# Sliding-window attention of a two-layer encoder step: the split of the transposed probabilities of every first tile goes from VectorE to GpSimd

## The chip, the cores and the metric

One core of a Trainium2 chip runs one launch of the whole step. The metric is the device time of that launch in microseconds. The kernel is one static program: every engine has its own list of instructions, written out in advance, and works through it in order; engines wait for each other by semaphores only.

## The reference, cut to what matters

A step of an encoder with one mLSTM layer and one layer of sliding-window attention, each followed by a SwiGLU feed-forward part, over 1024 prompt rows and 32 sample rows. The change lies in the attention of the second layer:

```python
def sink_attention(q, k, v, sinks, bias):
    s = jnp.einsum('bcqhgd,bckhd->bchgqk', q, k).astype(F32) * (HEAD_DIM ** -0.5) + bias
    sk = sinks.astype(F32).reshape(N_KV_HEADS, GROUP)[:, :, None, None]
    mx = jnp.maximum(jnp.max(s, -1, keepdims=True), sk)
    p = jnp.exp(s - mx)
    p = p / (jnp.sum(p, -1, keepdims=True) + jnp.exp(sk - mx))
    return jnp.einsum('bchgqk,bckhd->bcqhgd', p.astype(v.dtype), v)
```

There are 16 query heads of 64 dimensions, 2 shared key/value heads, chunks of 64 rows, and a window of 192 keys. Everything is float32. TensorE multiplies in the rounded format fp32r, so the kernel splits each operand x into hi = round(x) and lo = x - hi, and multiplies both halves.

## The kernel before, in words

The attention is a static software pipeline over 72 tiles (j, b). j = 0..7 is a couple of query heads, b = 0..8 a block of 128 rows (b = 8 holds the 32 sample rows). Tiles (j, b) with j even and j + 1 with the same b form a pair; j even is the first tile of a pair. The order is by visits (jp, g), each visit being heads j = 2 jp and 2 jp + 1 and three blocks b: first all four jp with g = 0, then for each jp the two other groups. The last visits are (3, 1) and (3, 2), so the last twelve tiles are (6,3), (7,3), (6,4), (7,4), (6,5), (7,5), (6,6), (7,6), (6,7), (7,7), (6,8), (7,8).

A tile passes six stages:

- `scores` (lines 1881 to 1910): TensorE multiplies query halves with key halves into the bank psS (L1898); VectorE adds the bias and takes a minimum (L1904).
- `soft` (L1919): ScalarE takes the exponential and its sum.
- `scale`: VectorE takes the reciprocal (L1929); GpSimd multiplies the tile of 128x384 by it (L1932; blocks 0 and 8 have L1936 in its place).
- `turn` (lines 1946 to 1962): TensorE transposes the three 128x128 pieces into a PSUM bank T (L1957, two banks); ScalarE copies them, rounded, into hi (L1961); VectorE subtracts hi from T into lo (L1962).
- `values` (L1986): once per pair, TensorE multiplies hi and lo of both tiles with the values into the PSUM bank O (one bank).
- `place`: once per pair, ScalarE copies half of O (L2000), VectorE adds it into the activations (L2004).

`pipeline` (lines 106 to 130) fixes the order in which these are written into the engines' lists. In one round it tries `place`, `turn`, `scale`, `soft`, `scores`, `values`, in that order; `turn` runs three tiles behind `scale`, and `values` one tile behind `turn`. So a round that turns tile k next scales tile k + 3; the values of a pair are multiplied in the round that turns the first tile of the following pair, and placed in the round after it. Blocks 0 and 8 are split in two narrower cuts per tile.

Between these stages `Weave` puts other work, by pauses in microseconds written into the code: projections of queries (L435 to L437 into d, L1750 and L1753 split them into Q), the splitting of the attention output for the output projection (`split_act`, L465 rounds, L466 subtracts; for the first group of columns the rounding of even k and the subtraction of odd k are on GpSimd), the splitting of weights (`Weights._next`, L256 and L258 round, L260 subtracts; for the output projection of this layer some halves are on GpSimd), and the first tiles of the output projection (L1272). None of these pauses depends on what an engine really takes, so the order of the lists does not change with the change below.

Of the kernel before, what the change touches and what calls it, by code (L numbers as in the profile page):

```python
# [9 lines left out]
F32 = mybir.dt.float32  # L10
# [6 lines left out]
P = 128  # L17
# [287 lines left out]
def kernel(ctx: ExitStack, tc: tile.TileContext, A, O):  # L305
    nc = tc.nc
# [5 lines left out]
    def pool(name, space=None, side=None):  # L312
        kw = {}
        if space is not None:
            kw["space"] = space
        if side is not None:
            kw["side"] = side
        return tc.tile_pool(name=name, bufs=1, reuse_waits="tile", **kw)

    def new(p, tag, shape, dt=F32, bufs=1):  # L320
        uid[0] += 1
        return p.tile(list(shape), dt, name=f"{tag}_{uid[0]}", tag=tag, bufs=bufs)
# [1498 lines left out]
    pb2 = eb.enter_context(pool("pb2"))  # L1821
# [47 lines left out]
    def attention():  # L1869
# [68 lines left out]
        def blocks(b):  # L1938

            if b == 0:  # L1940
                return [(1, 130, 64), (2, 258, P)]
            if b == 8:
                return [(0, 2, P), (1, 130, DEC)]
            return [(t, 2 + t * P, P) for t in range(3)]

        def turn(j, b):
            s = S.pop((j, b))
            p = s["p"]
            rows = 2 * DEC if b == 8 else P
            if j % 2 == 0:  # L1950
                pairs_[j // 2, b] = {
                    tag: new(pb2, tag, [P, 2, 3, P], F32R, bufs=2) for tag in ("hi", "lo")
                }
            s = pairs_[j // 2, b]
            pt = new(psb, "T", [P, 512], bufs=2).rearrange("p (t r) -> p t r", t=4)
            for t, at, nk in blocks(b):
                nc.tensor.transpose(pt[:nk, t, :rows], p[:rows, at : at + nk], ident[:rows, :rows])  # L1957
            cuts = [(slice(0, 3), P)] if 0 < b < 8 else [(slice(t, t + 1), nk) for t, _, nk in blocks(b)]
            hi, lo = (s[x][:, j % 2] for x in ("hi", "lo"))
            for t, nk in cuts:  # L1960
                nc.scalar.copy(hi[:nk, t, :rows], pt[:nk, t, :rows])  # L1961
                nc.vector.tensor_sub(lo[:nk, t, :rows], pt[:nk, t, :rows], hi[:nk, t, :rows].bitcast(F32))  # L1962
# [25 lines left out]
        def place(j, b):  # L1988
# [12 lines left out]
            for h in range(2):  # L2001
# [10 lines left out]
                (soft, always, 0, 0),  # L2012
                (scale, always, 0, 0),
                (turn, always, 2, gaps[0]),
                (values, lambda j, b: ast["v"] > b, 1, gaps[1]),
                (place, always, 0, 0),
# [201 lines left out]
```

## Time and profile before

| | before |
|---|---|
| median of 3 runs | 2192.62 us (2192.11 to 2194.38) |
| profiled execution | 2192.83 us, of which the span of the trace is 2190.7 us |
| granted TensorE clock over the span | 0.998 of full speed |
| busy share of the span: PE, PEld, DVE, ACT, POOL | 99%, 98%, 66%, 45%, 41% |
| instructions | 44028 |

PE is the matrix multiply of TensorE, PEld its loading of weights, DVE is VectorE, ACT is ScalarE and POOL is GpSimd. Times in the rows are microseconds from the start of the span unless marked ns. The attention runs from about 1206 to 1406 us; nothing of the change lies outside of it.

### The profile page before, as it was taken

The numbers are of one execution on the slowest core, as the hardware profiler recorded it, in microseconds if no ns is written. First come the engines' busy times: TensorE is split into PE (matmuls) and PEld (weight loads), VectorE is DVE, ScalarE is ACT, GpSimd is POOL, SyncE is SP. The second block draws the span as 40 slices with busy tenths as digits, with TensorE's granted clock in tenths as the row PEclk, the third lists the DMA queues.
The fourth block names the chain that finished last, engine by engine and source line by source line (L and its number), as shares of the span: only waits on it lengthen the run. The fifth ranks groups of instructions, "written<-read, shape, count | busy, mean of one in ns | idle before, by whom it ended". The sixth has DMA issues, their size and how long they took to land.

```text
span 2190.7 us, 44028 instructions
## 1 busy us (share of the span) xinstructions
PE 2162.7 (99%) x16982; PEld 2136.5 (98%) x16982; DVE 1455.3 (66%) x2833; ACT 991.9 (45%) x2234; POOL 903.3 (41%) x926
## 2 busy tenths in 40 slices
PE   9999999999999999999999999999999999999997
PEld 9999999999999999999999999999999999999997
DVE  4465676778767666466657776888666666457657
ACT  4443355455444444322235777656444444422125
POOL 2544210003655655454421443501665655554441
PEclk9999999999999999999999999999999999999999
DMA  5221112212656555697517433511443433397712
GB/s 172 75 66 55 51 49 80 96 40 69 235 197 208 211 201 200 205 333 252 180 45 245 150 118 126 161 35 39 145 146 143 158 140 143 131 358 244 254 52 80
DMA packets 187361, 322.49 MB, mean 147 GB/s; under 512 B 18768, under 2 KB 124296, under 8 KB 187152
## 3 DMA queue, kind: packets, MB, share of 16 engines
q1 hardware_dynamic: 182800, 315.36, 43.1%
q10 hardware_dynamic: 4352, 4.33, 0.6%
q8 instruction: 134, 2.20, 0.4%
q14 instruction: 75, 0.61, 0.1%
HBM read 221.23 MB, written 96.57 MB: 145 GB/s over the span
## 4 chain that ended last, share of the span: by engine, by line
PE 86%; DVE 7%; ACT 3%; issue 1%; DMA 1%; POOL 0%; SPq 0%; DVEq 0%; ACTq 0%; POOLq 0%
PE d L435 10%; PE A L435 10%; PE A L437 10%; PE A L436 10%; PE d L437 10%; PE d L436 10%; PE B L435 7%; PE B L436 7%; PE B L437 7%; PE O L1986 1%; PE psS L1898 1%; PE T L1957 1%; DMA hs_x<-z 1%; ACT act L538 1%; PE T L988 1%
## 5 line engine op out<-in xcount | busy, mean ns | idle before, releaser
L260 POOL TENSOR_TENSOR wl_s<-wr,wh_s 128x512 fp32r<-128x512 f32 x224 | 304.2, 1367 | 241.2 <-ACT wh_s L258 181.4
L435 PE MATMUL d<-sx,wh 128*128 128x264 f32 (+2 forms) x1040 | 331.4, 319 | 0.2
L260 POOL TENSOR_TENSOR wl_a<-wr,wh_a 128x512 fp32r<-128x512 f32 x112 | 155.7, 1392 | 401.9 <-ACT wh_a L258 397.7
L437 PE MATMUL d<-sx,wl 128*128 128x264 f32 (+2 forms) x1040 | 316.2, 304 | 1.7 <-DVE wl L260 0.9
L436 PE MATMUL d<-sx,wh 128*128 128x264 f32 (+2 forms) x1040 | 315.7, 304 | 0.6 <-DVE sx L466 0.4
L435 PE MATMUL A<-sx,wh_s 128*128 128x264 f32 x896 | 254.5, 284 | 0.0
L436 PE MATMUL A<-sx,wh_s 128*128 128x264 f32 x896 | 254.2, 284 | 0.0
L437 PE MATMUL A<-sx,wl_s 128*128 128x264 f32 x896 | 254.0, 284 | 0.0
L258 ACT CAST wh_s<-wr 128x512 fp32r<-128x512 f32 x224 | 135.7, 618 | 192.1 <-DVE wr L201 102.9
L435 PEld LDWEIGHTS d<-sx,wh 128*128 128x128 f32 x1040 | 196.0, 188 | 3.6 <-ACT sx L465 0.4
L436 PEld LDWEIGHTS d<-sx,wh 128*128 128x128 f32 x1040 | 196.3, 189 | 1.9 <-DVE sx L466 1.1
L437 PEld LDWEIGHTS d<-sx,wl 128*128 128x128 f32 x1040 | 195.5, 188 | 2.4 <-DVE wl L260 1.4
L435 PE MATMUL d<-sx,ex 128*128 128x264 f32 x624 | 180.7, 290 | 0.1
L436 PE MATMUL d<-sx,ex 128*128 128x264 f32 x624 | 177.2, 284 | 0.0
L437 PE MATMUL d<-sx,ex 128*128 128x264 f32 x624 | 176.9, 284 | 0.0
L437 PEld LDWEIGHTS A<-sx,wl_s 128*128 128x128 f32 x896 | 168.8, 188 | 0.0
L435 PEld LDWEIGHTS A<-sx,wh_s 128*128 128x128 f32 x896 | 168.4, 188 | 0.2 <-issue 0.2
L436 PEld LDWEIGHTS A<-sx,wh_s 128*128 128x128 f32 x896 | 168.4, 188 | 0.0
L1396 POOL TENSOR_TENSOR z<-z 128x528 fp32r<-128x528 f32 x76 | 103.9, 1367 | 122.6 <-ACT z L1395 114.1
L435 PE MATMUL A<-ex,wh_s 128*128 128x264 f32 x448 | 127.5, 285 | 0.0
L436 PE MATMUL A<-ex,wh_s 128*128 128x264 f32 x448 | 127.1, 284 | 0.0
L437 PE MATMUL A<-ex,wl_s 128*128 128x264 f32 x448 | 127.1, 284 | 0.0
(377 smaller groups left out, 7126.6 us busy)
## 6 DMA issues: line engine op xcount, KB each, us to landing
wr<-in_gu SPq DMA_DIRECT2D x92, 512.0 KB, 4.4
hs_x<-z SPq DMA_DIRECT2D x72, 528.0 KB, 3.1
hs_t<-z SPq DMA_DIRECT2D x64, 528.0 KB, 4.7
sx<-hs_x SPq DMA_DIRECT2D x112, 264.0 KB, 5.9
sx<-hs_t SPq DMA_DIRECT2D x64, 264.0 KB, 6.1
ex<-hs_t SPq DMA_DIRECT2D x64, 264.0 KB, 6.0
wr<-in_dn SPq DMA_DIRECT2D x32, 512.0 KB, 4.9
wh<-halves SPq DMA_DIRECT2D x38, 256.0 KB, 3.2
```

Source lines behind the costliest of these rows:

```text
L258: self.nc.scalar.copy(hi, r)
L260: eng.tensor_sub(lo, r, hi.bitcast(F32))
L435: nc.tensor.matmul(out, ah, bh, start=start and k == 0, stop=False, **kw)
L436: nc.tensor.matmul(out, ah, bl, start=False, stop=False, **kw)
L437: nc.tensor.matmul(out, al, bh, start=False, stop=stop and k == last, **kw)
L538: nc.scalar.activation(z, z, AF.Identity, scale=gk, bias=bk)
L988: nc.tensor.matmul(pc[:, : 2 * (DV + 1)], keys, vt[j][:, c], start=True, stop=True)
L1396: eng.tensor_sub(lo.bitcast(F32R), buf(s), hi)
L1898: nc.tensor.matmul(ps[:rows, at : at + nk], lhs, k[:, k0 : k0 + nk], start=i == 0, stop=i == 1)
L1957: nc.tensor.transpose(pt[:nk, t, :rows], p[:rows, at : at + nk], ident[:rows, :rows])
L1986: nc.tensor.matmul(out, v[:nk], x, start=i == 0, stop=i == len(todo) - 1)
```

## The change

For the first tile of each pair, in blocks 1 to 7 (4 x 7 = 28 of the 72 tiles), ScalarE copies the transposed probabilities out of PSUM as plain float32 into a new SBUF buffer "tc" (one buffer of 128x384). GpSimd then rounds that buffer into hi and subtracts hi from it into lo. ScalarE's rounding copy and VectorE's subtraction of these tiles are left out. The second tile of each pair and blocks 0 and 8 stay as they were.

```diff
             cuts = [(slice(0, 3), P)] if 0 < b < 8 else [(slice(t, t + 1), nk) for t, _, nk in blocks(b)]
             hi, lo = (s[x][:, j % 2] for x in ("hi", "lo"))
+            if j % 2 == 0 and 0 < b < 8:
+                c = new(pb2, "tc", [P, 3, P])
+                nc.scalar.copy(c[:], pt[:, :3])
+                nc.gpsimd.tensor_copy(hi[:], c[:])
+                nc.gpsimd.tensor_sub(lo[:], c[:], hi[:].bitcast(F32))
+                return
             for t, nk in cuts:
                 nc.scalar.copy(hi[:nk, t, :rows], pt[:nk, t, :rows])
                 nc.vector.tensor_sub(lo[:nk, t, :rows], pt[:nk, t, :rows], hi[:nk, t, :rows].bitcast(F32))
```

## Rows read from the trace of the kernel before

**Rows 1.** The page, part 1: busy time and share of the span.

```profile
PE 2162.7 (99%) x16982; PEld 2136.5 (98%) x16982; DVE 1455.3 (66%) x2833; ACT 991.9 (45%) x2234; POOL 903.3 (41%) x926
```

**Rows 2.** Busy time by stretch: attention, its tail (stretch, length, PE, PEld, DVE, ACT, POOL, clock, DMA).

```profile
1206.00:1410.00 204.00, 197.83 (x1457) 188.25 (x1456) 152.00 (x601) 148.20 (x495) 94.90 (x151) 1.00 0.42 131
...
1376.00:1406.00 30.00, 28.94 (x233) 27.87 (x234) 26.88 (x82) 23.25 (x70) 22.85 (x25) 1.00 0.49 146
```

**Rows 3.** Waits of TensorE, 1206 to 1410: waited for, total us, times, longest.

```profile
PE O L1986 <- DVE act L2004: 1.8, 4, 0.7
...
PEld T L1957 <- POOL s L1932: 1.2, 1, 1.2
```

**Rows 4.** Groups by shape, GpSimd, 1206 to 1410 (busy us, mean ns, idle before).

```profile
L1932 POOL TENSOR_TENSOR s<-s,st 128x384 f32<-128x384 f32 x56 | 47.6, 852 | 77.5 <-DVE st L1929 56.1 <-DVE st L1904 8.7 <-ACT s L1919 5.8
L466 POOL TENSOR_TENSOR sx<-act,sx 128x384 fp32r<-128x384 f32 x8 | 8.1, 1012 | 3.2 <-ACT sx L465 3.1
...
L465 POOL CAST sx<-act 128x384 fp32r<-128x384 f32 x4 | 2.0, 502 | 0.0
```

**Rows 5.** Groups by shape, 1200 to 1420: the split of VectorE and ScalarE.

```profile
L1962 DVE TENSOR_TENSOR lo<-T,hi 128x384 fp32r<-128x384 f32 x56 | 31.1, 556 | 12.5 <-ACT hi L1961 11.7
...
L1961 ACT CAST hi<-T 128x384 fp32r<-128x384 f32 x56 | 26.5, 476 | 15.0 <-PE T L1957 14.4
```

**Rows 6.** Timeline of GpSimd in the tail (start, us, instruction, idle before it).

```profile
1378.91 1.32 POOL L1932 TENSOR_TENSOR s<-s,st 128x384 f32<-128x384 f32 x1
...
1384.37 2.07 POOL L1932 TENSOR_TENSOR s<-s,st 128x384 f32<-128x384 f32 x2
...
1387.94 0.83 POOL L1932 TENSOR_TENSOR s<-s,st 128x384 f32<-128x384 f32 x1 [0.53 <-DVE st L1929]
1389.05 0.83 POOL L1932 TENSOR_TENSOR s<-s,st 128x384 f32<-128x384 f32 x1 [0.28 <-PE d L436]
...
1395.14 2.06 POOL L1932 TENSOR_TENSOR s<-s,st 128x384 f32<-128x384 f32 x2
1397.16 0.80 POOL L466 TENSOR_TENSOR sx<-act,sx 128x288 fp32r<-128x288 f32 x1
```

**Rows 7.** Timeline of TensorE in the tail.

```profile
1386.17 0.49 PE L1957 MATMUL T<-ident,s 128*128 128x128 f32 x3
...
1396.47 0.55 PE L1957 MATMUL T<-ident,s 128*128 128x128 f32 x3 [0.98 <-POOL s L1932]
...
1397.58 0.28 PE L1986 MATMUL O<-hi,VR 128*128 128x256 f32 x1
...
1401.16 0.28 PE L1986 MATMUL O<-hi,VR 128*128 128x256 f32 x1
```

**Rows 8.** Timeline of GpSimd, two roundings that VectorE waits for.

```profile
1273.69 0.83 POOL L1932 TENSOR_TENSOR s<-s,st 128x384 f32<-128x384 f32 x1 [0.42 <-DVE st L1929]
1274.46 0.50 POOL L465 CAST sx<-act 128x384 fp32r<-128x384 f32 x1
...
1283.73 0.50 POOL L465 CAST sx<-act 128x384 fp32r<-128x384 f32 x1
```

**Rows 9.** Timeline of VectorE behind those two roundings.

```profile
1275.00 0.56 DVE L466 TENSOR_TENSOR sx<-act,sx 128x384 fp32r<-128x384 f32 x1 [0.94 <-POOL sx L465]
...
1284.26 0.56 DVE L466 TENSOR_TENSOR sx<-act,sx 128x384 fp32r<-128x384 f32 x1 [1.40 <-POOL sx L465]
...
1286.12 0.85 DVE L2004 TENSOR_TENSOR act<-O,t 64x256 f32<-64x256 f32 x2
```

**Rows 10.** Timeline of TensorE: the value products behind them.

```profile
1276.46 0.35 PE L1986 MATMUL O<-hi,VR 128*128 128x256 f32 x1 [0.72 <-DVE act L2004]
...
1287.56 0.28 PE L1986 MATMUL O<-hi,VR 128*128 128x256 f32 x1
```

**Rows 11.** Line 1986, all its instructions: the semaphore row (ns min/median/max).

```profile
L1986 PEldq EVENT_SEMAPHORE  x28: 51/51/51, 1225.9 to 1404.2; - x28
```

**Rows 12.** Line 260, a row of its instructions: ns min/median/max, first and last start.

```profile
L260 DVE TENSOR_TENSOR wl<-wr,wh x53: 660/684/1287, 5.0 to 1519.8; 128x512 fp32r<-128x512 f32 x53
```

## The prediction

> **What bounds the kernel now.** I read the busy table first: TensorE's multiplies are busy for 99% of the span [rows 1], so time can be won only where TensorE waits, and is lost wherever something makes it wait. The table by stretch then says how much that is in the attention: PE is busy 197.83 of 204 us, so 6.2 us of idle time are all that any relief of another engine could give back there. It also says who has room. Over the whole attention GpSimd is busy 94.90 us of 204, less than half. In the last 30 us it is busy 22.85, and VectorE 26.88 [rows 2]. An average over the attention would hide that tail.
>
> Next the waits of TensorE. They are short and come from several engines: the longest sum is the value products behind VectorE's addition of the pair before (1.8 us in 4 waits), and there is one wait of 1.2 us for GpSimd's scaling [rows 3]. That last one is at 1396.47 [rows 7], in the tail, and is the warning: there GpSimd is already the engine that ends last.
>
> **What the change removes.** 28 of the 56 VectorE subtractions of 128x384 at 0.556 us go: 28 x 0.556 = 15.6 us of VectorE. 28 ScalarE roundings at 0.476 us become 28 plain copies of the same shape out of the same bank [rows 5]; I take the same duration, so zero. T becomes free one step earlier, after ScalarE. What are the 15.6 us worth? At most the 6.2 us of idle PE. I looked at what VectorE did just ahead of each wait that it ended: an addition, the query split, a reduction, or the subtraction of the second tile of a pair, which stays. In none was it the removed one. I take 0, and allow up to 2 us for shifts that I did not see.
>
> **What it adds.** 28 roundings and 28 subtractions of 128x384 on GpSimd. Both shapes exist: 0.502 and 1.012 us [rows 4]. Together 1.51 us per pair and 28 x 1.51 = 42.4 us, so GpSimd goes from 94.9 to 137 of 204 us. It has room on average; the question is what stands behind the 1.51 us in its list. By the order of a round, that is the scaling of tile k + 3, when tile k is turned, and whatever weight or activation splitting is woven in there.
>
> In the steady part this is covered. The scaling is needed only three tiles later, and a pair takes about 200 / 36 = 5.5 us. GpSimd stood idle for 77.5 us just ahead of its scalings [rows 4], which takes the delay up. The halves of the first tile are used by the values of its pair a whole pair's time later. So 22 or 23 of the 28 cost nothing as long as that idle time stands.
>
> **First place where it does not: two roundings.** At 1274.46 and 1283.73 GpSimd rounds activations [rows 8] for a subtraction in which VectorE already waits 0.94 and 1.40 us [rows 9]. Behind it stands the addition that frees the bank O for the next value products. In the list the new work of tile (6,2) goes ahead of a scaling just before the first rounding, that of (0,7) ahead of the scaling just before the second. Only 0.42 us of idle stood there in the first case [rows 8], so the rounding moves by 1.51 - 0.42 = 1.1 us, and TensorE, already waiting at 1276.46 [rows 10], by the same. In the second the rounding moves by about 1.5, but the addition ended at 1286.12 + 0.85 = 1286.97 and the products began at 1287.56 [rows 9, 10]: 0.6 us of slack, so 0.9 us. Together 2.0 us. Bounds: 0, if the new pieces start early enough, to 3.
>
> **Second place: the tail.** From about 1377 on GpSimd runs nearly without a gap. The work of (6,3) goes in ahead of the scaling at 1378.91, that of (6,4) between the two scalings at 1384.37, that of (6,5) ahead of the scaling at 1389.05. Three pieces make 3 x 1.51 = 4.5 us. GpSimd's gaps on the way are 0.53 and 0.28 us [rows 6]. So the first scaling at 1395.14, of tile (6,7), comes 4.5 - 0.8 = 3.7 us later. TensorE waited for it already, 0.98 us at 1396.47 [rows 7], so nothing is left to cover it: 3.7 us. A part falls due earlier: the first of the two scalings at 1384.37 ended at 1384.37 + 2.07 / 2 = 1385.4 and would end at 1386.9, against its transposes at 1386.17, a stall of about 0.75 us inside the 3.7. Then the piece of (6,6) stands between the two scalings at 1395.14 (1.03 each) and ends at 1396.2 + 3.7 + 1.5 = 1401.4, against value products due at 1397.58 + 3.7 = 1401.3; that of (6,7) follows the second scaling, the subtraction at 1397.16 and a narrower scaling that I put at 0.8 too, and ends near 1401.4 + 1.0 + 0.8 + 0.8 + 1.5 = 1405.5, against products due at 1401.16 + 3.8 = 1405.0 [rows 6, 7]. With 0.1 and 0.4 us the tail comes to 4.2 us. Bounds: 2, if only the last wait counts and something behind takes it up, to 6, from the next part.
>
> **Beside GpSimd, VectorE.** An operation of GpSimd next to a VectorE operation with two SBUF operands is stretched on both sides in this trace: the scaling takes 0.85 us in the mean and 1.32 at 1378.91, the weight subtraction 0.684 in the median and 1.287 at most [rows 4, 6, 12]. The subtraction removed reads PSUM and one SBUF tile; so do VectorE's score reductions. The new GpSimd pieces are long and can meet the two-operand ones: five pieces in the tail at 0.4 us each would be 2 us more. [...] I keep 4.2, because the scaling's mean is far below 1.32, so most pieces should run undisturbed, and the removed subtractions shorten VectorE's list at the same places.
>
> **Semaphores.** The values now wait for GpSimd besides ScalarE and VectorE. One more wait instruction per pair is 0.051 us [rows 11]: 0 if it hides behind the loading of weights, 28 x 0.051 = 1.4 us if not. I take 0.
>
> **Sum.** 2.0 + 4.2 = 6.2 us on the profiled execution of 2192.83, so 2199.0. The median is 0.2 us lower than that execution: 2198.8. About 0.2%, 4.4 us, is what a measurement of this kernel can tell from no change.
>
> **Rivals.**
>
> A. All is hidden (chance 0.34). GpSimd has 109 us to spare, and the pieces fit the gaps; ScalarE's earlier release of T and a lighter VectorE pay for what is left in the tail. For it: scalings lead by three tiles. Against it: the two places above. It gives 2192.6 plus 0 to 4.
>
> B. VectorE's relief decides (0.06). If most of TensorE's idle time was really VectorE's backlog, all 6.2 us could go: 2186.4. It decides from the point where over 4.4 of the 6.2 us come back. Against it: no wait that VectorE ended follows the removed subtraction, and the 1.2 us behind GpSimd grow.
>
> C. ScalarE is held up as well (0.16). There is one buffer "tc", so its next copy waits for GpSimd's subtraction of the pair before. When GpSimd is 3 us behind, ScalarE stands still at that copy, and with it the exponentials and the rounding of the second tile, for which the values wait. In the tail this happens at (6,5) and (6,7), with 0.6 to 2 us each; with the stretch above, the tail grows to 7 or 8 us: 2192.6 + 2 + 8 = 2202.6.
>
> **How the numbers follow.** The forecast proper (GpSimd's list delays the scaling in the tail and the two roundings) has 0.44, C 0.16: slower 0.60. A makes same 0.34, B faster 0.06. The likeliest gives 2198.8. Its bounds are 2 + 0 and 6 + 3 with 1.4 for semaphores and -2 for VectorE: 2192.6 to 2203.0. That takes in most of A and a good half of C; about 0.2 is left outside.
>
> **What would show it.** Right: GpSimd busy about 42 us more in the attention, L1962 at 28 of 128x384; waits of the transposes for L1932 several times 1.2 us, most of it after 1384; the subtraction L466 on VectorE waiting longer for the rounding; waits of TensorE elsewhere unchanged. Wrong: TensorE's idle time in the tail as before (then A), or long waits of ScalarE's plain copy for GpSimd (then C), or the waits for L2004 gone (then B). If GpSimd's pieces take much less than 1.51 us, the sum falls in proportion.

## The result and the profile after

The kernel with the change takes 2200.88 us in the median (2200.26 to 2201.29), the kernel before, run beside it, 2192.41 us (2192.11 to 2194.38): a ratio of 1.0037, 95% interval 1.0026 to 1.0047. That is 8.5 us slower; 6.2 were forecast. The spans of the two profiled executions differ by 2199.1 - 2190.7 = 8.4 us, so the traces can be compared step by step. In the kernel after, L1962 is ScalarE's plain copy, L1963 and L1964 GpSimd's rounding and subtraction, L1967 and L1968 the old pair for the second tiles, L1992 the value products, L2010 the addition.

The page after, part 1, answers to [rows 1]:

```profile
PE 2166.2 (99%) x16982; PEld 2139.6 (97%) x16982; DVE 1441.5 (66%) x2805; ACT 993.6 (45%) x2234; POOL 946.5 (43%) x982
```

GpSimd has 43.2 us and 56 instructions more, VectorE 13.8 us and 28 instructions less. PE has the same 16982 matmuls and is busy 3.5 us longer. The same work that takes longer is the first sign that more than waiting is at play.

Busy time by stretch after (columns as in [rows 2]: behind the five engines stand the granted clock, the DMA share and GB/s):

```profile
1206.00:1410.00 204.00, 192.72 (x1389) 182.98 (x1389) 133.62 (x557) 142.29 (x478) 133.23 (x203) 0.98 0.40 126
1376.00:1406.00 30.00, 25.30 (x202) 24.29 (x202) 20.99 (x74) 21.53 (x68) 28.47 (x32) 0.98 0.36 115
...
1278.00:1280.00 2.00, 1.78 (x9) 1.81 (x10) 0.68 (x7) 1.58 (x5) 1.60 (x3) 0.60 0.93 306
1280.00:1282.00 2.00, 2.00 (x11) 2.00 (x11) 1.71 (x4) 0.80 (x2) 1.86 (x5) 0.55 0.23 69
...
1404.00:1406.00 2.00, 2.00 (x13) 1.75 (x11) 0.00 (x0) 0.81 (x3) 1.92 (x4) 0.67 0.74 244
1406.00:1408.00 2.00, 2.00 (x12) 2.00 (x10) 1.97 (x4) 1.11 (x3) 2.00 (x3) 0.50 0.16 25
```

Over the whole attention GpSimd still has a third of the time free. In the last 30 us it is busy 28.47 (before 22.85), while PE falls from 28.94 to 25.30 and VectorE from 26.88 to 20.99 [rows 2]. VectorE has less to do there and waits more; and since the kernel after is 3.5 to 8 us behind there, the same 30 us also hold less of the work. The last four rows show what the prediction had no term for. The granted clock of TensorE, 1.00 in both stretches of [rows 2], falls to 0.60 and 0.55 after 1278 and to 0.67 and 0.50 after 1404. Read in stretches of 0.5 us from 1206 to 1418, it is 1.00 but for two dips: 0.50 from 1278.5 to 1281.5 and from 1405.0 to 1408.0, with one stretch of 0.68 to 0.90 at each end. So the numbers between are stretches that were partly at 1.00. In 1406 to 1408 PE is busy all the time and gets through 12 matmuls; at a clock of 1.00 it gets through 20 in such a stretch (the version with two fills, below).

Waits after, 1206 to 1418 (columns as in [rows 3]):

```profile
DVE sx L466 <- POOL sx L465: 7.5, 4, 3.4
...
ACT tc L1962 <- POOL lo L1964: 7.2, 3, 4.5
...
PE T L1957 <- POOL s L1932: 4.3, 2, 3.5
...
PE O L1992 <- DVE act L2010: 3.3, 6, 1.8
...
PEld O L1992 <- POOL lo L1964: 0.2, 1, 0.2
```

TensorE's own waits for GpSimd's scaling are 4.3 us in two (one of 0.98 us before [rows 7]), and those for the addition 3.3 us in place of 1.8 [rows 3]. The first and second rows name two engines that wait for GpSimd's new work. Which of them matters is a matter of experiments: the wait of 7.2 us on ScalarE turns out to cost nothing. The two longest of the first row stand at the roundings of [rows 8] (timeline of VectorE after):

```profile
1276.17 0.56 DVE L466 TENSOR_TENSOR sx<-act,sx 128x384 fp32r<-128x384 f32 x1 [2.49 <-POOL sx L465]
...
1287.56 0.56 DVE L466 TENSOR_TENSOR sx<-act,sx 128x384 fp32r<-128x384 f32 x1 [3.43 <-POOL sx L465]
```

They were 0.94 and 1.40 us [rows 9]; the additions that free the bank O stand behind them.

Groups by shape after, 1206 to 1418 (columns as in [rows 4, 5]):

```profile
L1932 POOL TENSOR_TENSOR s<-s,st 128x384 f32<-128x384 f32 x56 | 47.1, 840 | 54.3 <-DVE st L1929 35.5 <-DVE st L1904 8.7 <-PE psS L1898 3.2
L1964 POOL TENSOR_TENSOR lo<-tc,hi 128x384 fp32r<-128x384 f32 x28 | 28.4, 1013 | 2.3
L1963 POOL CAST hi<-tc 128x384 fp32r<-128x384 f32 x28 | 15.5, 555 | 3.1 <-ACT tc L1962 2.6
...
L1962 ACT COPY tc<-T 128x384 f32<-128x384 f32 x28 | 13.3, 474 | 13.6 <-POOL lo L1964 7.2 <-PE T L1957 4.9 <-POOL s L1936 0.9
```

A pair costs GpSimd 1.013 + 0.555 = 1.57 us, 43.9 us over 28 pairs (1.51 and 42.4 were forecast). The plain copy takes 474 ns against 476 of the rounding copy, so ScalarE gains nothing. GpSimd's idle time ahead of its scalings shrinks from 77.5 [rows 4] to 54.3 us: more than half of the new work disappears in it.

Timeline of TensorE after (start, us, instruction, idle before it and its releaser):

```profile
1274.25 0.49 PE L1957 MATMUL T<-ident,s 128*128 128x128 f32 x3
...
1277.63 0.36 PE L1992 MATMUL O<-hi,VR 128*128 128x256 f32 x1 [1.79 <-DVE act L2010]
...
1281.84 0.49 PE L1957 MATMUL T<-ident,s 128*128 128x128 f32 x3
...
1286.29 0.49 PE L1957 MATMUL T<-ident,s 128*128 128x128 f32 x3
...
1290.42 0.36 PE L1992 MATMUL O<-hi,VR 128*128 128x256 f32 x1 [0.30 <-DVE act L2010]
...
1293.96 0.33 PE L1957 MATMUL T<-ident,s 64*128 64x64 f32 x2
...
1387.76 0.49 PE L1957 MATMUL T<-ident,s 128*128 128x128 f32 x3
...
1390.58 0.55 PE L1957 MATMUL T<-ident,s 128*128 128x128 f32 x3 [0.78 <-POOL s L1932]
...
1403.68 0.55 PE L1957 MATMUL T<-ident,s 128*128 128x128 f32 x3 [3.51 <-POOL s L1932]
...
1405.80 0.41 PE L1992 MATMUL O<-lo,VZ 128*128 128x256 f32 x1
1406.02 0.41 PE L1992 MATMUL O<-hi,VZ 128*128 128x256 f32 x1
...
1408.16 0.49 PE L1957 MATMUL T<-ident,s 128*128 128x128 f32 x3
```

The same of before, beside those of [rows 7] and [rows 10]:

```profile
1274.15 0.49 PE L1957 MATMUL T<-ident,s 128*128 128x128 f32 x3
...
1279.09 0.49 PE L1957 MATMUL T<-ident,s 128*128 128x128 f32 x3
...
1290.59 0.33 PE L1957 MATMUL T<-ident,s 64*128 64x64 f32 x2
...
1384.30 0.49 PE L1957 MATMUL T<-ident,s 128*128 128x128 f32 x3
...
1399.28 0.49 PE L1957 MATMUL T<-ident,s 128*128 128x128 f32 x3
```

Held against each other, these rows give the loss as it grows:

| instruction | before | after | later by |
|---|---|---|---|
| transposes ahead of the first rounding | 1274.15 | 1274.25 | 0.10 |
| value products behind the first rounding | 1276.46 [rows 10] | 1277.63 | 1.17 |
| next transposes | 1279.09 | 1281.84 | 2.75 |
| transposes ahead of the second place | 1283.91 | 1286.29 | 2.38 |
| value products behind the second rounding | 1287.56 [rows 10] | 1290.42 | 2.86 |
| transposes behind them | 1290.59 | 1293.96 | 3.37 |
| transposes of (7,4), 15 tiles with the change later | 1384.30 | 1387.76 | 3.46 |
| transposes of (6,5) | 1386.17 [rows 7] | 1390.58 | 4.41 |
| value products ahead of those of (6,7) | 1392.59 | 1397.26 | 4.67 |
| transposes of (6,7) | 1396.47 [rows 7] | 1403.68 | 7.21 |
| transposes of (7,7) | 1399.28 | 1408.16 | 8.88 |

Two places make the loss: 3.37 - 0.10 = 3.3 us around 1276 to 1292, and 8.88 - 3.46 = 5.4 us from 1386 on. The 90 us between them add 0.1; what lies ahead of 1274 and behind 1418 adds about 0.4 and takes back about 0.5. In the first, 1.58 us (1.17 to 2.75) grow behind the wait, while PE is busy at the lower clock; in the second 1.67 us (7.21 to 8.88), of which 0.25 is one more wait, of a weight load for GpSimd's subtraction (the last of the waits above), and 1.4 the clock. The value products of 128x256 follow each other there every 0.22 us (1405.80, 1406.02), against 0.12 before, at a clock of 1.00 (the products at 1397.82 and 1397.94).

### The profile page after: what moved, and what is told of

Same layout as the page of the kernel before. It is cut to its first block, busy times and chain, and to the rows that moved or that the text cites. A ratio compares the mean times of both kernels' runs of the same rounds, so it can differ in the third digit from the quotient of the medians.

```text
span 2199.1 us, 44075 instructions
## 1 busy us (share of the span) xinstructions
PE 2166.2 (99%) x16982; PEld 2139.6 (97%) x16982; DVE 1441.5 (66%) x2805; ACT 993.6 (45%) x2234; POOL 946.5 (43%) x982
## 4 chain that ended last, share of the span: by engine, by line
PE 86%; DVE 6%; ACT 3%; DMA 2%; POOL 2%; issue 1%; SPq 0%; POOLq 0%; ACTq 0%; DVEq 0%
PE d L435 10%; PE d L437 10%; PE d L436 10%; PE A L435 10%; PE A L437 9%; PE A L436 9%; PE B L435 7%; PE B L436 7%; PE B L437 7%; PE O L1992 1%; PE psS L1898 1%; DMA hs_x<-z 1%; DMA sx<-hs_t 1%; ACT act L538 1%; PE T L988 1%
## 5 line engine op out<-in xcount | busy, mean ns | idle before, releaser
L1396 POOL TENSOR_TENSOR z<-z 128x528 fp32r<-128x528 f32 x76 | 104.5, 1375 | 121.1 <-ACT z L1395 108.4
```

The source lines that it names most:

```text
L1396: eng.tensor_sub(lo.bitcast(F32R), buf(s), hi)
```

## The experiments

Time is the median, with the kernel before beside it on the same chip: 2192.09 us for the first four, 2191.81 for the next four, 2192.05 for the last two. The theory: GpSimd's list, longer by the new pieces, delays the two roundings and the scaling of (6,7), and nothing else costs. The rivals: the other 21 tiles or VectorE's relief also count, ScalarE's hold-up at the single buffer "tc" counts, or the loss in the tail comes from something other than lateness of GpSimd.

**Tail taken back.** The last pairs, from (6,3) on, are split as before.

```diff
-            if j % 2 == 0 and 0 < b < 8:
+            if j % 2 == 0 and 0 < b < 8 and not (j == 6 and b >= 3):
```

> The change without its last five tiles (6,3) to (6,7). Theory (GpSimd's list delays two places only): TensorE's shift up to 1376 us stays at about 3.4 us, the tail adds nothing: 2195.8 us (2195.0 to 2196.8), and the clock dip after 1404 is gone. Rival (the price is spread over all 28 tiles, as work or semaphores): 23/28 of 8.5 us = 7.0, so 2199.4. Rival (one buffer tc holds ScalarE everywhere): also near 2199.

Measured: 2195.60 us, 1.0017 [1.0007, 1.0026], 3.5 us above before. TensorE's waits in its timeline:

```profile
1279.43 0.36 PE L1992 MATMUL O<-hi,VR 128*128 128x256 f32 x1 [1.81 <-DVE act L2010]
...
1401.08 0.55 PE L1957 MATMUL T<-ident,s 128*128 128x128 f32 x3 [0.98 <-POOL s L1932]
```

and a stretch behind the first of them:

```profile
1280.00:1282.00 2.00, 1.98 (x16) 2.00 (x17) 0.48 (x5) 1.78 (x5) 1.80 (x3) 1.00 0.88 308
```

The wait for the scaling of (6,7) is back at 0.98, as before [rows 7]. The first place stands by itself with a wait of 1.81 us, and here the clock stays at 1.00 behind it: the dip after a wait of this length is not bound to come.

**The two roundings taken back.** Only the tiles (6,2) and (0,7) are split as before.

```diff
-            if j % 2 == 0 and 0 < b < 8:
+            if j % 2 == 0 and 0 < b < 8 and (j, b) not in ((6, 2), (0, 7)):
```

> The change without the tiles (6,2) and (0,7). Theory: the 3.4 us shift between 1274 and 1291 is gone, clock dip at 1278 to 1282 included, the tail keeps about 5.4: 2197.8 us (2197.0 to 2198.8). Rival (spread over all tiles): 26/28 of 8.5 = 7.9, so 2200.3. Rival (the dip comes by itself, not from the wait behind the rounding): still about 1.7 us at 1278, so 2199.3.

Measured: 2197.43 us, 1.0026 [1.0015, 1.0036], 5.3 us above before. The wait at the first place is 0.72 us again, as in [rows 10]; in the tail the waits are 0.78 and 3.51 us, the same as with the whole change. The clock around the second is not the same:

```profile
1398.00:1400.00 2.00, 0.34 (x2) 0.34 (x3) 0.00 (x0) 0.00 (x0) 2.00 (x3) 0.57 0.76 248
1400.00:1402.00 2.00, 2.00 (x11) 2.00 (x10) 0.00 (x0) 0.84 (x3) 1.92 (x4) 0.50 0.80 254
```

This wait ends at 1399.66, so the clock fell while TensorE still stood. It stays at 0.50 up to 1404, longer than the 3.4 us (1404.7 to 1408.1) in the tail of the kernel after, and behind the wait this trace loses 2.4 us where the kernel after loses 1.7. The two places add up, 3.5 + 5.3 = 8.8 against 8.5 us, but only roughly, as the 2.4 and 1.7 us behind the same wait of 3.51 us show.

**Both taken back.** 21 of the 28 tiles keep the change.

```diff
-            if j % 2 == 0 and 0 < b < 8:
+            if j % 2 == 0 and 0 < b < 8 and not (j == 6 and b >= 2) and (j, b) != (0, 7):
```

> The change without (6,2) to (6,7) and (0,7): 21 tiles keep it. Theory: those 21 cost and gain nothing: 2192.4 us (2191.9 to 2193.2). Rival (spread): 21/28 of 8.5 = 6.4, so 2198.8. Rival (VectorE's relief of 21 x 0.556 = 11.7 us is worth something once the two places are out): below 2191.5.

Measured: 2192.10 us, 1.0000 [0.9991, 1.0010]. Three quarters of the change cost nothing and gain nothing that shows: 21 x 1.57 = 33 us of GpSimd are hidden, and 21 x 0.556 = 11.7 us taken off VectorE are worth nothing. The interval leaves room for 2 us either way; in the trace TensorE falls back by 0.4 us over the attention.

**A second buffer "tc" in the tail.** Space that the prologue uses is taken again for the copies of (6,4) and (6,6), so that ScalarE need not wait for GpSimd's subtraction of the pair before. The lines that take the space in the prologue are left out here.

```diff
+                if j == 6 and b in (4, 6):
+                    c = cc[:, : 3 * P].rearrange("p (t r) -> p t r", t=3)
+                else:
+                    c = new(pb2, "tc", [P, 3, P])[:]
```

> The change with a second buffer for the plain copies of (6,4) and (6,6), so that ScalarE's copies of (6,5) and (6,7) no longer wait for GpSimd's subtraction of the pair before (2.34 and 4.46 us in the trace). Theory: GpSimd is busy without a gap there, so its list and not ScalarE sets the end: within 0.5 us of 2200.9. Rival C (ScalarE held up counts): 2 to 4 us less, 2197 to 2199.

Measured: 2201.18 us, 1.0042 [1.0027, 1.0057], the same as with the change. Of ScalarE's wait of 7.2 us for GpSimd 1.2 are left; it waits longer for the transposes instead (8.7 us, 4.9 with the change), and TensorE's waits for the scaling are 0.78 and 3.7 us. ScalarE stood still beside the path, not on it.

**GpSimd only subtracts.** ScalarE makes the plain and the rounded copy.

```diff
-                nc.gpsimd.tensor_copy(hi[:], c[:])
+                nc.scalar.copy(hi[:], pt[:, :3])
```

> All 28 tiles, but ScalarE makes both the plain copy and the rounded hi, and GpSimd only subtracts: 1.01 in place of 1.57 us on GpSimd per tile, 0.48 us more on ScalarE. Theory (GpSimd's list): the scaling of (6,7) comes 3 x 1.01 - 0.8 = 2.2 us late in place of 3.7, the two roundings move by 0.6 and 1.0: 2195.3 us without a clock dip, up to 2197.5 with one after the long wait. Rival (any tile pays, in proportion to GpSimd's time): 2192.1 + 8.8 x 0.64 = 2197.7. Rival (ScalarE is the engine that matters): slower than the change itself, over 2201.

Measured: 2199.47 us (2197.80 to 2201.01), 1.0033 [1.0022, 1.0044], 7.7 us above before: outside of what was expected. Timeline of TensorE:

```profile
1400.96 0.55 PE L1957 MATMUL T<-ident,s 128*128 128x128 f32 x3 [2.40 <-POOL s L1932]
...
1406.72 0.35 PE L1992 MATMUL O<-hi,VR 128*128 128x256 f32 x1 [0.91 <-DVE act L2010]
```

GpSimd's part shrank as it should: the wait of (6,7) is 2.40 us in place of 3.51, and TensorE is 2.1 us further behind at these transposes than at 1384, where 2.2 were expected. But 1.8 us more come behind it, most of them at a new wait of 0.91 us for an addition. ScalarE, with 28 x 0.483 = 13.5 us more, is busy 24.11 of the 30 us from 1376 to 1406 (21.53 with the change), but its half of O for that addition was ready at 1404.2. What stands just ahead of the addition (at 1405.73) in VectorE's own list is this (timeline of VectorE):

```profile
1403.72 2.09 DVE L260 TENSOR_TENSOR wl<-wr,wh 128x512 fp32r<-128x512 f32 x1
```

This weight subtraction takes 0.684 us in the median [rows 12]; here, beside a GpSimd that runs without a gap (busy all of 1402 to 1406), it takes 2.09. It also starts late, behind a wait of 3.40 us for a rounding of ScalarE's, which had itself stood still 2.76 us for GpSimd's subtraction of the pair before. Which of the two made the wait was not separated. The profiled execution (2198.11 us) shows no dip of the clock (1.00 over 1206 to 1418). The mean granted clock of the whole launch is 0.998 in it and 0.997 in four of the five slower ones, a hint that those had one.

**GpSimd held up by itself.** To the kernel before, with none of the change, six fills of 128x512 are added on GpSimd ahead of the scaling of (6,7); in a second version two. This measures the disputed term alone: what does TensorE lose when this one scaling is late?

```diff
+                if (j, b) == (6, 7):
+                    for _ in range(6):
+                        nc.gpsimd.memset(new(pb2, "hold", [P, 512])[:], 0.0)
```

> The kernel before with six fillings of a scratch tile on GpSimd (about 0.56 us each, 3.4 in all) ahead of the scaling of tile (6,7), and nothing else. It adds work that is not in the reference's computation. Theory (that scaling is on TensorE's path, and the long wait brings the clock down behind it): 3.4 us plus a dip of about 1.7: 2197.2 us, granted clock near 0.5 for some us behind the wait. Rival (the slow products after 1404 come from the new hi and lo buffers, not from the wait): 3.4 us alone, 2195.5, clock at 1. Rival (the delay is taken up behind the attention): 2192.1.

> The same with two fillings (1.1 us in all), a wait of about 2.1 us in place of 4.4. Work is added that is not in the reference's computation. Theory: 1.1 us without a dip, 2193.2; with one up to 2194.9. Rival (taken up behind): 2192.1.

Measured: six fills 2197.04 us, 1.0022 [1.0013, 1.0032], 5.2 above before; two fills 2192.64 us, 1.0004 [0.9994, 1.0013], 0.8 above before. The waits came out shorter than expected (3.90 and 1.57 us, not 4.4 and 2.1): the fills take 3.4 and 1.1 us as written, but the scaling behind them takes 0.83 us, where it took 1.27 before. The version with six in the timeline of TensorE:

```profile
1398.42 0.55 PE L1960 MATMUL T<-ident,s 128*128 128x128 f32 x3 [3.90 <-POOL s L1935]
```

and by stretch:

```profile
1398.00:1400.00 2.00, 1.58 (x9) 1.58 (x10) 0.43 (x1) 0.94 (x3) 2.00 (x4) 0.71 0.00 0
1400.00:1402.00 2.00, 2.00 (x11) 2.00 (x10) 1.24 (x4) 0.39 (x1) 1.51 (x2) 0.50 0.40 78
```

The version with two in the same views:

```profile
1396.38 0.55 PE L1960 MATMUL T<-ident,s 128*128 128x128 f32 x3 [1.57 <-POOL s L1935]
```

```profile
1398.00:1400.00 2.00, 2.00 (x20) 2.00 (x19) 1.90 (x6) 1.23 (x3) 1.49 (x2) 1.00 0.45 81
```

A late scaling alone does what the tail of the change does. The wait grows from 0.98 to 3.90 us, 2.9 longer. From there to the next transposes 1.5 us more are lost at a clock of 0.71 and 0.50. With a wait of 1.57 us the clock stays at 1.00 and the loss is the 0.6 us of waiting. So the price of lateness is not proportional: behind the longer wait a second charge comes due, 1.5 us in this execution. It is the fastest of the ten (2195.79 us); by the median, 5.2 - 2.9, the charge is 2.3 us.

**Room for GpSimd.** The change on all 28 tiles, with the weights that GpSimd splits in the tail given to ScalarE and VectorE, and its roundings of activations (four in this group, [rows 4]) to ScalarE.

```diff
-    on_vector.update((u, 0) for u in U_OUT_B[0][EARLY:])
-    W = Weights(nc, base, units, pairs, on_vector, {(u, 1) for u in U_OUT_B[0][EARLY:]})
+    on_vector.update((u, f) for u in U_OUT_B[0][EARLY:] for f in range(2))
+    W = Weights(nc, base, units, pairs, on_vector, set())
...
-                    (nc.gpsimd.tensor_copy, nc.scalar.copy),
+                    (nc.scalar.copy, nc.scalar.copy),
```

> The change on all 28 tiles, and GpSimd's other splitting taken away: the five weight halves of the tail rounded on ScalarE and subtracted on VectorE, the roundings of the first column group on ScalarE. Theory (what stood around the new work was the trouble, the work itself is free where GpSimd has room): the wait of 1.2 us at 1396 and the waits for the four roundings go: 2190.5 us (2189.5 to 2192.2). Rival (VectorE becomes the bound in the tail, five subtractions of 0.69 us more against five of 0.556 less): 2193 to 2196.

Measured: 2195.96 us, 1.0018 [1.0009, 1.0027], 4.2 above before: the rival held. TensorE's timeline in the tail:

```profile
1375.57 0.36 PE L1898 MATMUL psS<-KH,Q 128*128 128x192 f32 x1 [1.63 <-DVE st L1904]
...
1395.12 0.35 PE L1992 MATMUL O<-hi,VR 128*128 128x256 f32 x1 [1.59 <-DVE act L2010]
```

and a stretch behind the last wait:

```profile
1398.00:1400.00 2.00, 2.00 (x11) 2.00 (x11) 1.75 (x4) 0.47 (x2) 2.00 (x3) 0.51 0.00 0
```

The waits for GpSimd are gone, and two waits of 1.6 us for VectorE stand in their place; the clock falls behind the second of them (0.51) and not behind the first, where the value products follow each other every 0.12 us (1376.49, 1376.61). In the tail VectorE has no room for this work either. But between 1296 and 1375 the transposes of this run stood 1.6 us earlier than those of before, and only 0.4 at the start of the attention: without GpSimd's roundings 1.2 us are gained even with the change, at two waits for the addition, one of 0.60 us at 1265.89 before and the one of 0.72 in [rows 10]. That led to the last two runs.

**What is left when the losses are avoided.** One kernel keeps the change on 22 tiles, all but (6,2) to (6,7), and gives GpSimd's roundings to ScalarE (the same four as above); the other is the kernel before with that move of the roundings alone.

```diff
-            if j % 2 == 0 and 0 < b < 8:
+            if j % 2 == 0 and 0 < b < 8 and not (j == 6 and b >= 2):
...
-                    (nc.gpsimd.tensor_copy, nc.scalar.copy),
+                    (nc.scalar.copy, nc.scalar.copy),
```

> The change stays on the 22 first tiles up to the pair (6,1) and is taken back for the last six pairs; in the mixed group whose GpSimd roundings fall between 1260 and 1290 us both roundings are ScalarE's. Theory (GpSimd's lateness reaches TensorE only where GpSimd stands between two engines that wait, which were the roundings and the scaling of (6,7)): with the roundings off GpSimd nothing is lost, and the 1.1 to 1.2 us that TensorE waited for them before (rows 9 and 10, and the offset of -1.2 us in the run with the relocated tail weights) come back: ratio about 0.9995, 0.8 to 1.5 us below the kernel before. Rival (ScalarE, with 28 eviction copies and two more roundings, is late itself): not below the kernel before, up to 2 us above.

> The kernel before with nothing but the two GpSimd roundings of that mixed group moved to ScalarE. Theory: the same 0.8 to 1.5 us below the kernel before, and within 0.3 us of the run with the change on 22 tiles, since the 15.6 us that the change takes off VectorE were worth nothing. Rival (VectorE's relief is worth something once GpSimd's roundings are out of the way): this run is slower than the other by 1 us or more.

Measured: 2190.55 us, 0.9993 [0.9984, 1.0002], with the change on 22 tiles; 2190.21 us, 0.9991 [0.9982, 1.0000], without it: 1.5 and 1.8 us below before, the second a little more than expected. Neither trace has TensorE's waits of before at 1265.89 and 1276.46 any more. The difference to before is at the edge of what the intervals tell. Between the two it is 0.3 us, in favour of the kernel without the change: what is gained comes from the four roundings, and the relief of VectorE adds nothing to it that would show.

## Why the prediction was right, and where its sizes were off

The direction, the two places and the waits in them were right; the time was 2.1 us short (2198.8 forecast, 2200.88 measured), inside the range of 2192.6 to 2203.0. Step by step:

- **VectorE's relief, 0.** Right, within the 2 us that the intervals leave open. The version with 21 tiles stands at 1.0000, and the last two runs differ by 0.3 us the other way.
- **GpSimd, 1.51 us per pair, hidden in 22 or 23 of 28.** Measured 1.57. The subtraction came as read from the row (1.013 against 1.012), the rounding is slower by 0.05 us in the mean. 21 tiles are shown to be hidden; in the trace no product waits for (6,7) either, which makes 22.
- **First place, 1.1 + 0.9 = 2.0 us.** The first wait grew by 1.79 - 0.72 = 1.07 us, as forecast. At the second the delay grows from 2.38 to 3.37, 1.0 us, as forecast too. The place cost 3.3 us in the trace, because 1.58 us were added at the lower clock between the two, of which 2.75 - 2.38 = 0.37 came back before the second. In the trace with the tail taken back, which has no dip there, the same two steps are 1.15 and 1.55 us (0.37 of the second a wait for a weight's transfer), 2.7 in all. So the dip adds between 3.3 - 2.7 = 0.6 and 1.58 - 0.37 = 1.2 us to this place; more closely it is not settled.
- **Tail, 4.2 us.** Measured 5.4. The list of GpSimd, with the three pieces where the prediction put them (timeline of GpSimd after):

```profile
1382.37 0.96 POOL L1963 CAST hi<-tc 128x384 fp32r<-128x384 f32 x1
...
1384.38 1.17 POOL L1932 TENSOR_TENSOR s<-s,st 128x384 f32<-128x384 f32 x1
...
1390.47 0.73 POOL L1963 CAST hi<-tc 128x384 fp32r<-128x384 f32 x1
...
1394.79 0.96 POOL L1963 CAST hi<-tc 128x384 fp32r<-128x384 f32 x1
...
1399.25 1.69 POOL L260 TENSOR_TENSOR oh<-wr,oh 128x512 fp32r<-128x512 f32 x1
...
1402.80 0.83 POOL L1932 TENSOR_TENSOR s<-s,st 128x384 f32<-128x384 f32 x1
```

  The scaling of (6,7) moved from 1395.14 [rows 6] to 1402.80, 7.66 us, of which 3.46 was there before the tail: 4.2 us late by itself, against 3.7 forecast. The roundings are stretched here, 0.96, 0.73 and 0.96 us in place of 0.50, and one weight subtraction to 1.69 us in place of 1.29. Each of the four lies beside an operation of VectorE with two SBUF operands, the second beside one of 0.98 us at 1389.86, the fourth beside one of 0.68 us at 1399.12, the first and the third beside these (timeline of VectorE after):

```profile
1382.28 0.69 DVE L260 TENSOR_TENSOR wl<-wr,wh 128x512 fp32r<-128x512 f32 x1
...
1394.57 0.81 DVE L260 TENSOR_TENSOR wl<-wr,wh 128x512 fp32r<-128x512 f32 x1 [0.27 <-ACT wh L258]
```

  That is the stretch that the prediction weighed and left out. No run tried by itself what causes it. In the net it is worth about 0.5 us here, not the 2 us that the prediction put on it: from start to start the three pieces take 5.8 us, 1.3 more than forecast, but the rest of the list, stretched at other places before, takes 0.8 less. TensorE's waiting grew by 4.41 - 3.46 = 0.95 at (6,5), 0.26 behind it, and 7.21 - 4.67 = 2.54 at (6,7), together 3.75 us; with the 0.25 us of the weight load 4.0. Of the 0.1 and 0.4 us that were put on value products behind GpSimd's pieces, the first is that 0.25, and the second did not come: no product of the last pair waits for GpSimd.
- **Missing term: the clock behind a long wait.** 1.4 us in the tail, and the fills show 1.5 (2.3 by their median) without any of the change. With it the tail is 4.0 + 1.4 = 5.4 us, where the sum of the waits alone comes within 0.2 us of the forecast. This is the size that was off: the prediction took a wait of TensorE to cost its own length.
- **Semaphores, 0.** Nothing in the 21 tiles speaks for more; 21 x 0.051 = 1.1 us would not stand out from their interval, but their trace has 0.4 us for everything.
- **Rival A** failed at the two places it had against it. **Rival B** had the sign wrong: the waits for the addition grew from 1.8 to 3.3 us. **Rival C** saw a real wait of ScalarE (4.5 us at most), and was refuted by the second buffer: the products it would delay stand behind the late scaling anyway. Its time, 2202.6, is 1.7 us off, closer than the forecast's 2.1, for the wrong reason; the time alone could not have told them apart.

## What to carry to other kernels

An engine with half its time free is not free where its list stands between two engines that already wait: find the releasers of the bound engine's waits, follow them back through what they wait for, and price the new work in those lists, ahead of those waits alone. The rest of it cost nothing that showed here, and taking work off an engine at places where no such wait stands behind it gained nothing. A wait of the bound TensorE can cost more than its length: behind the 3.90 us of the six fills 1.5 us more were lost at a clock of 0.71 and 0.50, behind the 1.57 us of the two fills the clock stayed at 1.00 and the loss was the 0.6 us of waiting. Where two engines both have no room in a stretch, as in this tail, work is only passed round; leaving it where it was, or taking off the list the work that the others wait for (here four roundings, worth 1.5 to 1.8 us at the edge of the intervals), is what helped.

## What was not expected of the hardware

TensorE's granted clock fell to 0.50 around waits of 3.51 us (the kernel after, and with the two roundings taken back), of 3.7 us (with the second buffer "tc") and of 3.90 us (six fills), and came back to 1.00 while TensorE went on without a pause: in the kernel after at 1408.1, with PE busy all the time from 1404 to 1410. With the two roundings taken back it fell while TensorE still stood (0.57 in 1398 to 1400, with the wait up to 1399.66), in the others within two microseconds behind the wait (in the kernel after at 1404.7, behind a wait up to 1403.68). It stayed at 1.00 behind waits of 0.98 us (before), 1.57 us (two fills) and 2.40 us (GpSimd only subtracts). Around waits of 1.6 to 1.8 us it went either way: it fell behind 1.79 us (0.55), 1.8 us (0.50, with the second buffer) and 1.59 us (0.51), and stayed at 1.00 behind 1.81 us and, by the pace of the value products, behind 1.63 us. So the length of the one wait does not decide alone; no run here tried what does.

The other find is a weight subtraction of 128x512 on VectorE that took 2.09 us beside a GpSimd without a gap, in the run in which GpSimd only subtracts. The median before is 0.684 us and the longest 1.287 [rows 12].
